# Modulation at one step a half unit beside GLA, one more half unit for the first GLA head, and the DFT table loaded by ScalarE

## The chip, the cores and the metric

The kernel runs on one core of a Trainium2 chip. The metric is the device time of one execution in microseconds (us); smaller is better. TensorE (PE) multiplies, VectorE (DVE) and ScalarE (ACT) work element by element, GpSimd (POOL) and SyncE (SP) here mostly issue DMAs. All engines run at the same time, each through its own list of instructions in order, and wait for each other by semaphores.

## The reference, cut to what matters

One layer of a hybrid diffusion backbone on 384 tokens (128 of context, 256 latent) of width 2048, in float32:

```python
mod = silu(cond) @ w_ada + b_ada          # six maps: shift, scale, gate, twice
h = rmsnorm(x) * (1 + sc1) + sh1
q, k, v, g, lr_f, lr_b, fo = split(h @ w_in)
o = gla(q, k, v, decay(lr_f)) + flip(gla(flip ..., decay(lr_b)))   # 4 heads, 6 chunks of 64
o = rmsnorm(o) * norm * silu(g)
f = real(fft2(fo))                         # over positions and 256 channels, 4 groups
g_a, g_b = split(sigmoid(h @ w_gate + b_gate))
m = (g_a * (o @ w_br_gla) + g_b * (f @ w_br_four)) @ w_out
x = x + ga1 * rmsnorm(m)
h = rmsnorm(x) * (1 + sc2) + sh2
x = x + ga2 * rmsnorm((silu(h @ w_ffn_gate) * (h @ w_ffn_up)) @ w_ffn_down)
```

Two of the six modulation maps are made at the start; the other four (adaLN, `w_ada`) are made beside the matrix products.

## The kernel before

Activations lie transposed, 16 blocks of 128 features by 384 tokens. To keep float32 accuracy, every weight tile (`raw`, 128x1024) is split in two: ScalarE casts it to `whi` (L301; L292 and L295 for special tiles), and VectorE subtracts to get `wlo` (L288, with the shared `TENSOR_TENSOR` operation). A product is then three matmuls (L327: hi by hi, hi by lo, lo by hi). A **half unit** is one weight tile's worth of them: 24 matmuls. A projection of 128 output columns is two half units (`proj`). `grab()` takes the next split pair and, by `push()`, starts the loads and the split of a later one, so that the split runs some half units ahead; `depth[0]` says how many loads lie ahead.

The order on PE, ACT, DVE and POOL is the order in which the code is written; SP is not in that schedule, and its loads are issued as soon as a buffer is free. Work beside the products is written as generators, advanced by `step(side)` once a half unit:

- `gla()`: the scan of each of 4 heads, cut in some 14 steps: `kr`/`krs`, `z` and the log-decay `la` split into `lah`, `lal` (L379/L380), `bT` (L835) and its exponentials, `ki` (L852), the scores `at` (L875), the states `dl`, the outputs `po` (L789), with per-head sums of squares. After the last head, `rs` is taken (L941, L942) and the output is scaled (L946, twelve small operations in three steps).
- `ada_rest()`: the modulation maps in 6 parts. Each part takes 16 weight steps: POOL loads `adaw` (512 KB, 2 buffers), and DVE adds it into `adacc` with two operations (L708; L706 for the first). Then one empty step and one in which PE sums over partitions (`pr`, L719, 8 matmuls). While `on_pe[0]` is set, a weight step is instead four matmuls on PE (L698).
- `run_after()`: 14 turns beside the last seven gate projections (i = 25 to 31), the **folding stage**: sums and differences of token columns for the Fourier branch (`t` L727, `r` L732/L733, ACT copy L728, `hF` L739/L741), and weights of the Fourier columns, folded in place by DVE (L257, L258), with 16 matmuls a tile from the fourth turn on (`pfo`, L1040/L1041).
- in the following stage the output-gate columns ("o"), the DFT and the Fourier branch's projection (`four`, `pf` L1240/L1241) alternate; then come the merge ("a" and "b" tiles), `w_out`, norms and the feed-forward network.

`paced(gen, rate)` advances the modulation `rate[0]` steps a call; in the stage with q, k and 25 gate projections the rate is 1.07. `low_later` delays the `wlo` of a plain weight tile until the next split: DVE then does the folding work first. `cd` is the table of cosines and sines for the DFT (128x1934, 967 KB, L1063), first read by the `pp` matmuls (L1130) in the stage after. In the stage "o" a step of modulation is taken in turns 0 to 5 and then every second turn, on PE from turn 6; in the merge, `TAIL` names the "a" tiles with a step (True: on PE).

Of the kernel before, what the change touches and what calls it, by code (L numbers as in the profile page):

```python
# [37 lines left out]
XU = 2  # L38
GF = 25
GD = 256  # L40
TAIL = {1: True, 4: False, 5: True, 8: True, 10: False, 11: True, 14: False}
RATE = 1.07


C_TRI = 0
# [7 lines left out]
C_CE = C_SEL3 + 96  # L53
# [3 lines left out]
NC = C_CT + 2 * (HT + HL)  # L57
# [51 lines left out]
def tile_step(ctx: ExitStack, tc: tile.TileContext, a, o):  # L109
    nc = tc.nc  # L110
    PE, ACT, DVE, POOL, SP = nc.tensor, nc.scalar, nc.vector, nc.gpsimd, nc.sync
# [137 lines left out]
    low_later = [False]  # L249
# [61 lines left out]
    def take():  # L311
        return ready.pop(0)
# [371 lines left out]
    on_pe = [False]  # L684
# [50 lines left out]
    def over_parts(k, r, low):  # L735

        hi, lo = (hF[k // 4][:, k % 4 : k % 4 + 2, n, :] for n in range(2))
        if low:
            DVE.tensor_sub(lo, r, hi.bitcast(F32))  # L739
        else:  # L740
            ACT.copy(hi, r)  # L741
# [9 lines left out]
    rate = [1.0]  # L751
    ada_gen = ada_rest([(m, half) for m in (2, 3, 4) for half in range(2)])
    ada = paced(ada_gen, rate)
    with ExitStack() as s:
# [22 lines left out]
        def chunks(x):  # L777
            return x.rearrange("p (t c i) -> p t c i", t=3, c=2)

        def gla():  # L780
# [10 lines left out]
            for h in range(NH):  # L791
# [34 lines left out]
                yield  # L826
                if h == 0:
                    yield
                for d in range(2):


                    bT = pss.tile([P, T], F32, tag="side", name="bT")
                    for t in range(3):
                        for j, l in enumerate((lah, lal)):
                            PE.matmul(  # L835
                                bT[:, t * P : (t + 1) * P], l[:, t, d], tri[:, d * P : (d + 1) * P],
                                start=j == 0, stop=j == 1,
                            )
                    sx = pss.tile([P, 2, P], F32, tag="side", name="sx")
                    for j, l in enumerate((lah, lal)):  # L840
                        PE.matmul(
                            sx, tri[:, (2 + d) * P : (3 + d) * P], l[:, 0 : 2 + d : 1 + d, d], start=j == 0, stop=j == 1,
                        )
                    eb = pg.tile([P, T], F32, tag=f"eb{d}", name="eb")
                    ACT.activation(eb, bT, AF.Exp)
                    ki = pg.tile([P, T], F32, tag=f"ki{d}", name="ki")
                    ACT.activation(ki, bT, AF.Exp, scale=-1.0)
                    ko = pg.tile([P, 2, P], F32, tag=f"ko{d}", name="ko")
                    ACT.activation(ko, sx, AF.Exp)
                    qi = pg.tile([P, T], F32, tag=f"qi{d}", name="qi")  # L850
                    DVE.scalar_tensor_tensor(qi, eb, DK**-0.5, qT[:, h, :], op0=ALU.mult, op1=ALU.mult)
                    DVE.tensor_mul(ki, ki, kT[:, h, :])  # L852
                    DVE.tensor_mul(ko, ko, krs[:, 0 : 2 + d : 1 + d, :])

                    last = 0 if d else CH - 1
                    tot = chunks(eb)[:, :, d, last : last + 1]
                    kc = pg.tile([P, 3, CH], F32, tag=f"kc{d}", name="kc")
                    DVE.tensor_mul(kc, chunks(ki)[:, :, d, :], tot.to_broadcast([P, 3, CH]))
                    dc = pg.tile([P, 1], F32, tag=f"dc{d}", name="dc")
                    c = 5 if d else 2  # L860
                    e0, e1 = c * CH + last, (c + 1 - 2 * d) * CH + last
                    DVE.tensor_mul(dc, eb[:, e0 : e0 + 1], eb[:, e1 : e1 + 1])
                    qin.append(qi)
                    kin.append(ki)
                    kcr.append(kc)
                    kout.append(ko)
                    dec.append((tot, dc))
                    yield
# [100 lines left out]
        def side():  # L969
            while True:  # L970
                next(gl, None)
                next(ada, None)
                yield

        sd = side()
        rate[0] = RATE
        for i in qk_order[1:]:
            proj(psm, hT, keep(qk, i), sd)

# [35 lines left out]
    cd = px.tile([P, 2 * G], F32, tag="cd", name="cd")[:, 0 : NC - C_CE]  # L1015
    with ExitStack() as s:
        more = s.enter_context(tc.tile_pool(name="more", bufs=1))
        hF = [actp.tile([P, 4, 2, T], F32R, tag=t, name="hF") for t in ("C_lo", "B_hi", "B_lo")]
        hF.append(more.tile([P, 4, 2, T], F32R, tag="hF", name="hF"))
        sums, folds = [], {}  # L1020

        def ends(n):
            t, r = (more.tile([P, 2, T], F32, tag=z, name=z) for z in ("t", "r"))
            over_ends(2 * n, t, r)
            over_parts(2 * n, r, False)
            folds[n] = r

        def across_n(h, n):
            if n == 0:
                sums[:] = [pss.tile([P, 2, hi - lo], F32, tag="side", name="pfo") for _ in range(2) for lo, hi, _ in parts]  # L1030
            w = take()
            push()
            w_of = [x.rearrange("p (g i k c) -> p i k g c", g=2, i=2, k=2) for x in w]
            for k in range(2):
                kt = 2 * n + k
                x = hF[kt // 4][:, kt % 4]
                for g in range(2):
                    for i, (lo, hi, _) in enumerate(parts):
                        p = sums[2 * g + i]
                        PE.matmul(p, w_of[0][:, i, k, g, :], x[:, :, lo:hi], start=kt == 0, stop=False)  # L1040
                        PE.matmul(p[:, 0], w_of[1][:, i, k, g, :], x[:, 0, lo:hi], start=False, stop=kt == KT - 1)  # L1041
            if n == 7:
                for g in range(2):
                    X.append(px.tile([P, T], F32, tag="yb", name="X", bufs=4))
                    for i, (lo, hi, _) in enumerate(parts):
                        p = sums[2 * g + i]
                        ACT.copy(X[-1][:, lo:hi], p[:, 1])
                        DVE.tensor_add(X[-1][:, lo:hi], X[-1][:, lo:hi], p[:, 0])

        def run_after():  # L1050
            for at, todo in enumerate(after):
                for what, *n in todo:
                    if what == "ends":
                        ends(*n)
                    elif what == "parts":
                        over_parts(2 * n[0], folds.pop(n[0]), True)
                    else:
                        if n == [1, 5]:
                            depth[0] = 2
                            spare_raws.clear()  # L1060
                        across_n(*n)
                if at == turns // 2:
                    SP.dma_start(cd, a["consts"][:, C_CE:NC])  # L1063
                if at in (turns - 4, turns - 3, turns - 1):
                    next(ada_gen, None)
                yield

        ra = run_after()
        low_later[0] = True
        for i in range(GF, 32):  # L1070
            proj(psm, hT, gate(more, i), ra)
            if i == GF:
                depth[0] = 4
                spare_raws.extend([lambda: more.tile([P, G], F32, tag="raw3", name="raw3", bufs=2)] * 2)
        catch_up()
        low_later[0] = False
        depth[0] = 0
        xq = px.tile([P, HT], F32, name="xq")
        POOL.memset(xq, 0.0)
        qb = pss.tile([P, HT], F32, tag="side", name="pfq")  # L1080
        for kb in range(0, KT, 4):
            for x_ in range(2):
                for k in range(kb, kb + 4):
                    q = 32 * (k % 4)
                    PE.matmul(
                        qb[q : q + 4, :], wq[:, k, :], hF[k // 4][:, k % 4, x_, 0:HT].bitcast(F32),
                        start=kb == 0 and x_ == 0, stop=kb == KT - 4 and x_ == 1,
                    )
        for q in range(0, P, 32):
            ACT.copy(xq[q : q + 4, :], qb[q : q + 4, :])  # L1090
# [3 lines left out]
    with ExitStack() as s:  # L1094
# [83 lines left out]
        turn = [0]  # L1178

        def side():  # L1180
            while True:
                on_pe[0] = turn[0] > 5
                if turn[0] < 6 or turn[0] % 2:
                    next(ada_gen, None)
                on_pe[0] = False
                turn[0] += 1
                next(df, None)
                next(nw, None)
                yield
# [71 lines left out]
        for b, i in mix_order:  # L1261
# [18 lines left out]
            else:  # L1280
# [3 lines left out]
                if i == KT - 3:  # L1284
                    depth[0] = 2
                    spare_raws.clear()
                if i in TAIL:
                    on_pe[0] = TAIL[i]
                    next(ada_gen, None)
# [810 lines left out]
```

## Time and profile before

| | us |
|---|---|
| median of 3 runs (lowest, highest) | 1955.28 (1954.93, 1955.28) |
| the profiled execution's own time | 1954.75 |
| its span in the trace | 1953.0 |
| PE busy in the span | 1923.8 (99%) |
| DVE busy | 1650.9 (85%) |
| ACT busy | 915.7 (47%) |
| POOL busy | 85.8 (4%) |

By stages (PE busy of the stretch): start to 142 us: 133.7 of 135; q, k and 25 gate projections with GLA, 142 to 443: 296.8 of 301; folding stage, 443 to 548: 100.8 of 105 (DVE 91.7); stage "o", 548 to 670: 121.3 of 122; merge and `w_out`, 670 to 880: all of 210; the rest, 880 to 1953: 1058.5 of 1073.

A row of the timeline has the start and duration in us, engine, line, operation, output <- input, shapes and count; in brackets stands how long the engine was idle before it and what ended that. The chain of waits has start, duration, and what. In a table of windows, the column after the engines' busy times is the granted clock of TensorE (PEclk, 1 is full), then the DMA engines' share and their rate.

### The profile page before, as it was taken

Reading aid. Unit: us, or ns where it says so; the run is one execution under the profiler, and the core shown is the slowest. Engines: PE = TensorE matmul, PEld = TensorE weight load, DVE = VectorE, ACT = ScalarE, POOL = GpSimd, SP = SyncE. Lnnn points to the kernel's source line nnn. Section 1 sums busy time; section 2 is a strip of 40 time slices with the busy share of each in tenths; the row PEclk is TensorE's granted clock in tenths of the full one; section 3 lists DMA queues with packets and bytes.
Section 4 is the critical chain, followed back from the end, with each engine's and each line's share of the span. In section 5 each row is a group of like instructions: output and inputs, shape, how many; then the busy total and the mean of one; then the engine's idle time right before and its main releaser. Section 6 shows DMA issues by size and latency. Waiting matters only on the chain.

```text
span 1953.0 us, 27535 instructions
## 1 busy us (share of the span) xinstructions
PE 1923.8 (99%) x10526; PEld 1692.8 (87%) x10526; DVE 1650.9 (85%) x2174; ACT 915.7 (47%) x1298; POOL 85.8 (4%) x154
## 2 busy tenths in 40 slices
PE   8999999999999999999999999999999999999997
PEld 5779999999999999999988888888888888888876
DVE  5668898989868897987789898999998999888885
ACT  4235445544455644456454444444444444444444
POOL 0001111110000000004000000000000000000001
PEclk9999999999999999999999999999999999999999
DMA  9977766766556895656254635363636263625243
GB/s 390 387 257 240 252 223 230 261 233 219 181 161 227 297 310 190 222 195 220 81 176 148 189 109 190 126 207 110 205 109 215 93 221 92 200 76 183 86 168 112
DMA packets 200615, 380.52 MB, mean 195 GB/s; under 512 B 14196, under 2 KB 126932, under 8 KB 196132
## 3 DMA queue, kind: packets, MB, share of 16 engines
q1 hardware_dynamic: 181396, 321.83, 48.7%
q0 software_dynamic: 13952, 50.39, 8.5%
q10 hardware_dynamic: 5136, 6.56, 0.9%
q8 instruction: 82, 1.34, 0.3%
q14 instruction: 49, 0.40, 0.1%
HBM read 361.94 MB, written 16.78 MB: 194 GB/s over the span
## 4 chain that ended last, share of the span: by engine, by line
PE 71%; DVE 3%; DMA 1%; ACT 1%; issue 0%; ACTq 0%; DVEq 0%; SPq 0%
PE pgu L339 30%; PE pdn L339 18%; PE pmm L327 17%; PE pf L1240 1%; PE pmm L1517 1%; PE pfo L1040 1%; PE ptr L1809 1%; PE pf L1241 1%; DMA raw<-in_w_d 0%; DMA raw<-in_w_gate 0%; PE pfo L1041 0%; DVE adacc L708 0%; DVE x1b L1961 0%; DMA raw<-in_w_in 0%; PE pr L698 0%
## 5 line engine op out<-in xcount | busy, mean ns | idle before, releaser
L327 PE MATMUL pmm<-A_hi,wlo 128*128 128x384 f32 x1072 | 360.0, 336 | 4.2 <-DVE wlo L288 4.2
L327 PE MATMUL pmm<-A_hi,whi 128*128 128x384 f32 x1072 | 362.8, 338 | 0.0
L327 PE MATMUL pmm<-A_lo,whi 128*128 128x384 f32 x1072 | 359.6, 335 | 0.0
L1664 ACT CAST whi<-u 128x1024 fp32r<-128x1024 f32 x200 | 210.6, 1053 | 281.6 <-DVE u L1648 86.2
L1664 ACT CAST whi<-raw 128x1024 fp32r<-128x1024 f32 x175 | 184.2, 1052 | 202.0 <-PE pgu L339 59.4
L1675 DVE TENSOR_TENSOR wlo<-u,whi 128x1024 fp32r<-128x1024 f32 x200 | 244.3, 1222 | 31.5 <-ACT whi L1664 17.9
L339 PE MATMUL pgu<-whi,A_hi 128*128 128x512 f32 x640 | 250.0, 391 | 0.0
L339 PE MATMUL pgu<-whi,A_lo 128*128 128x512 f32 x640 | 249.3, 389 | 0.0
L1675 DVE TENSOR_TENSOR wlo<-raw,whi 128x1024 fp32r<-128x1024 f32 x175 | 213.7, 1221 | 38.5 <-ACT whi L1664 30.8
L288 DVE TENSOR_TENSOR wlo<-raw,whi 128x1024 fp32r<-128x1024 f32 x163 | 198.3, 1220 | 25.8 <-ACT whi L301 24.4
L301 ACT CAST whi<-raw 128x1024 fp32r<-128x1024 f32 x149 | 155.9, 1050 | 120.8 <-PE pmm L327 57.2
L327 PEld LDWEIGHTS pmm<-A_hi,wlo 128*128 128x128 f32 x1072 | 202.1, 188 | 4.9 <-DVE wlo L288 4.9
L327 PEld LDWEIGHTS pmm<-A_hi,whi 128*128 128x128 f32 x1072 | 202.1, 188 | 3.4 <-issue 2.5
L708 DVE SCALAR_TENSOR_TENSOR adacc<-adaw,spad,adacc 128x1024 f32<-128x1024 f32 x162 | 200.6, 1280 | 2.4 <-DMA adaw<-in_w_ada 1.9
L327 PEld LDWEIGHTS pmm<-A_lo,whi 128*128 128x128 f32 x1072 | 202.2, 189 | 0.2
L339 PE MATMUL pdn<-whi,hid_hi 128*128 128x512 f32 x480 | 186.9, 389 | 0.0
L339 PE MATMUL pdn<-whi,hid_lo 128*128 128x512 f32 x480 | 186.8, 389 | 0.0
L339 PE MATMUL pgu<-wlo,A_hi 128*128 128x512 f32 x640 | 184.2, 389 | 0.0
L339 PEld LDWEIGHTS pgu<-whi,A_hi 128*128 128x128 f32 x640 | 120.2, 188 | 26.1 <-issue 0.8
L339 PEld LDWEIGHTS pgu<-wlo,A_hi 128*128 128x128 f32 x640 | 120.1, 188 | 25.4
L339 PEld LDWEIGHTS pgu<-whi,A_lo 128*128 128x128 f32 x640 | 120.1, 188 | 25.0
L339 PE MATMUL pgu<-whi,S 128*128 128x512 f32 x480 | 131.1, 395 | 0.0
(405 smaller groups left out, 3042.7 us busy)
## 6 DMA issues: line engine op xcount, KB each, us to landing
adaw<-in_w_ada POOLq DMA_DIRECT2D x96, 512.0 KB, 3.9
raw<-in_w_d SPq DMA_DIRECT2D x88, 512.0 KB, 3.7
slab<-in_w_ada SPq DMA_DIRECT2D x32, 1024.0 KB, 10.0
raw<-in_w_gate SPq DMA_DIRECT2D x64, 512.0 KB, 4.6
raw<-in_w_g SPq DMA_DIRECT2D x48, 512.0 KB, 3.5
raw<-in_w_u SPq DMA_DIRECT2D x48, 512.0 KB, 3.6
raw<-in_w_in SPq DMA_DIRECT2D x44, 512.0 KB, 4.2
u<-in_w_u SPq DMA_DIRECT2D x40, 512.0 KB, 4.7
```

The costliest lines, as they stand in the source:

```text
L288: eng.tensor_sub(lo, raw, hi.bitcast(F32))
L301: ACT.copy(hi, raw)
L327: PE.matmul(dst, w[wi][:, k * n + n0 : k * n + n0 + P], x[xi][:, k0 + k, :], start=first and k == 0 and j == 0, stop=last and k == kts - 1 ...
L339: PE.matmul(dst, stat[x_][m], mov(w[w_], m), start=first and w_ == m == x_ == 0, stop=last and w_ == m == 1,)
L708: DVE.scalar_tensor_tensor(acc[:, c, :], w, spad[:, k, c : c + 1], acc[:, c, :], op0=ALU.mult, op1=ALU.add,)
L1040: PE.matmul(p, w_of[0][:, i, k, g, :], x[:, :, lo:hi], start=kt == 0, stop=False)
L1240: PE.matmul(pf[:, 0 : 2 * HT], w[0][:, c], x[k], start=k == 0, stop=False)
L1241: PE.matmul(pf[:, 0:HT], w[1][:, c], x[k][:, 0:HT], start=False, stop=m == 1 and k == 3)
L1517: PE.matmul(hp[u], hw[u][j][:, ((k - 1) % 8) * P : ((k - 1) % 8 + 1) * P], h2[m][:, k - 1, :], start=k == 1 and j == m == 0, stop=k == KT ...
L1664: ACT.copy(hi, src)
L1675: DVE.tensor_sub(lo, src, hi.bitcast(F32))
L1809: PE.transpose(pt[:, j, :], src[:, j * P : (j + 1) * P], ident)
```

## The change

- `RATE` goes: beside GLA the modulation takes one step a half unit.
- For head 0 `gla()` takes one more empty step after the split of the log-decay.
- The load of `cd` in turn 7 of the folding stage is issued by ACT, in its program order, instead of by SP.
- `low_later` is set after the first of the seven gate projections instead of before it.
- In the stage "o" the modulation's steps are taken in turns 0 to 8 and then in odd turns; they run on PE from turn 7 on, without turn 8.
- `TAIL` gets a step at tile 13 (on PE) and one at 15 (on DVE).

Counted over the program, there are 87 calls of the modulation ahead of `w_out` before and after; one of the weight steps more is on PE (10 instead of 9) and one fewer on DVE.

```diff
-TAIL = {1: True, 4: False, 5: True, 8: True, 10: False, 11: True, 14: False}
-RATE = 1.07
+TAIL = {1: True, 4: False, 5: True, 8: True, 10: False, 11: True, 13: True, 14: False, 15: False}
@@ gla()
                 split_act(lah, lal, la)
                 yield
                 if h == 0:
+                    yield
                     yield
@@
         sd = side()
-        rate[0] = RATE
         for i in qk_order[1:]:
             proj(psm, hT, keep(qk, i), sd)
@@ run_after()
                 if at == turns // 2:
-                    SP.dma_start(cd, a["consts"][:, C_CE:NC])
+                    ACT.dma_start(cd, a["consts"][:, C_CE:NC])
@@
         ra = run_after()
-        low_later[0] = True
         for i in range(GF, 32):
             proj(psm, hT, gate(more, i), ra)
             if i == GF:
                 depth[0] = 4
+                low_later[0] = True
                 spare_raws.extend([lambda: more.tile([P, G], F32, tag="raw3", name="raw3", bufs=2)] * 2)
@@ side() of the stage "o"
-                on_pe[0] = turn[0] > 5
-                if turn[0] < 6 or turn[0] % 2:
+                on_pe[0] = turn[0] > 6 and turn[0] != 8
+                if turn[0] < 9 or turn[0] % 2:
                     next(ada_gen, None)
```

Three places show how this moves instructions. First DVE, where the stage with GLA ends and the folding stage begins (L946 scales the GLA output; `raw` under L257 and L258 is the first Fourier weight). Before:

```order
L946 TENSOR_SCALAR qk<-qk,rs 128x2x128 x4
L708 SCALAR_TENSOR_TENSOR adacc<-adaw,spad,adacc 128x1024 x2
L946 TENSOR_SCALAR qk<-qk,rs 128x2x128 x4
L727 TENSOR_TENSOR t<-A_hi,A_lo 128x768
L732 TENSOR_TENSOR r<-t 128x2x64
L733 TENSOR_TENSOR r<-t 128x2x63
L732 TENSOR_TENSOR r<-t 128x2x128
L733 TENSOR_TENSOR r<-t 128x2x127
L257 TENSOR_TENSOR raw<-raw 128x2x256
L258 SCALAR_TENSOR_TENSOR raw<-raw 128x2x256
L288 TENSOR_TENSOR wlo<-raw,whi 128x1024
L739 TENSOR_TENSOR hF<-r,hF 128x2x384
```

After (line numbers in this part of the program are one smaller, except in `gla`):

```order
L707 SCALAR_TENSOR_TENSOR adacc<-adaw,spad,adacc 128x1024 x2
L946 TENSOR_SCALAR qk<-qk,rs 128x2x128 x8
L287 TENSOR_TENSOR wlo<-raw,whi 128x1024
L726 TENSOR_TENSOR t<-A_hi,A_lo 128x768
L731 TENSOR_TENSOR r<-t 128x2x64
L732 TENSOR_TENSOR r<-t 128x2x63
L731 TENSOR_TENSOR r<-t 128x2x128
L732 TENSOR_TENSOR r<-t 128x2x127
L256 TENSOR_TENSOR raw<-raw 128x2x256
L257 SCALAR_TENSOR_TENSOR raw<-raw 128x2x256
L738 TENSOR_TENSOR hF<-r,hF 128x2x384
```

The GLA output is finished one half unit later, and the `wlo` that stood behind the first turn's sums and the first fold now stands ahead of the first `t`.

Second, the load of `cd`. On SP before, at the start of the folding stage, ahead of a gate's weights:

```order
L235 DMA raw_4617<-in_w_in 128x4x256
L235 DMA raw_4619<-in_w_gate 128x1024
L1063 DMA cd<-in_consts 128x1934
L235 DMA raw<-in_w_gate 128x1024
L235 DMA raw<-in_w_in 128x4x256
```

On ACT after, in turn 7, some 40 us later in the program:

```order
L300 CAST whi<-raw_4810 128x1024
L727 COPY r<-t 128x2x2
L740 CAST hF<-r 128x2x384
L1062 DMA cd<-in_consts 128x1934
L259 COPY wq<-raw_4842 128x2x2
L291 CAST whi<-raw_4842 128x1024
L982 ACTIVATE gz<-pmm,bgate 128x384
```

SP's row is gone, and behind ACT's row stand the casts of a Fourier weight and of the next gate.

Third, ACT in the stage with GLA, at the log-decay of head 2 (`la`; `gz` is a finished gate tile, stored by the DMA behind it). Before:

```order
L301 CAST whi<-raw 128x1024
L983 ACTIVATE gz<-pmm,bgate 128x384
L984 DMA gates_d<-gz 128x384
L819 ACTIVATE la<-z 128x512
L819 ACTIVATE la<-z 128x256
L820 ACTIVATE la<-la 128x768
```

After:

```order
L300 CAST whi<-raw 128x1024
L982 ACTIVATE gz<-pmm,bgate 128x384
L983 DMA gates_d<-gz 128x384
L300 CAST whi<-raw 128x1024
L818 ACTIVATE la<-z 128x512
L818 ACTIVATE la<-z 128x256
```

Since every later GLA step of heads 0 to 3 falls one half unit later, the gate's `gz` and its DMA now stand one cast ahead of `la` instead of right ahead of it.

## Prediction

> **What bounds the kernel.** I read the page's engine shares first, then TensorE's waits, then the timeline at each long one, and for the longest the chain of waits and the granted clock.
>
> ```profile
> PE 1923.8 (99%) x10526; PEld 1692.8 (87%) x10526; DVE 1650.9 (85%) x2174; ACT 915.7 (47%) x1298; POOL 85.8 (4%) x154
> ...
> PE pmm L327 <- DVE wlo L288: 4.2, 2, 3.7
> ```
>
> PE is busy for 1923.8 of 1953.0 us. The change leaves the matmuls nearly as they are, so it can gain only from PE's waiting (29 us in all) and from time in which PE's clock is low. PE's longest wait in the stages that change is the 3.7 us for a `wlo`. These are the others there:
>
> ```profile
> 189.72 0.57 PE L875 MATMUL at<-qi,ki 128*64 128x64 f32 x12 [1.76 <-DVE ki L852]
> ...
> 223.98 0.64 PE L719 MATMUL pr<-adacc,selr 128*32 128x256 f32 x8 [0.91 <-DVE adacc L708]
> 225.18 0.64 PE L719 MATMUL pr<-adacc,selr 128*32 128x256 f32 x8 [0.56 <-DVE adacc L708]
> ...
> 317.15 0.33 PE L835 MATMUL bT<-cg,lal 128*128 128x128 f32 x1 [0.37 <-DVE lal L380]
> 384.16 0.33 PE L835 MATMUL bT<-cg,lal 128*128 128x128 f32 x1 [0.56 <-DVE lal L380]
> ...
> 532.34 0.44 PE L327 MATMUL pmm<-A_hi,wlo 128*128 128x384 f32 x1 [0.53 <-DVE wlo L288]
> 595.90 0.36 PE L1241 MATMUL pf<-edT,wlo 128*128 128x194 f32 x1 [0.66 <-DVE wlo L288]
> ```
>
> The long one lies at the start of the folding stage. Here are rows of the chain of waits, in order of time, and then three windows:
>
> ```profile
> 447.17 1.05 DVE qk L946 x4
> ...
> 451.71 1.23 DVE wlo L288
> ...
> 453.00 7.61 DMA raw<-in_w_gate
> ...
> 464.84 1.23 DVE wlo L288
> ...
> 466.12 6.67 PE pmm L327 x22
> ```
>
> ```profile
> 462.40:464.94 2.54, 0.00 (x1) 0.00 (x0) 2.07 (x5) 1.13 (x3) 0.00 (x0) 1.00 0.21 77
> 464.94:471.76 6.82, 5.64 (x18) 5.64 (x19) 6.75 (x11) 3.35 (x6) 0.00 (x0) 0.50 0.50 154
> ...
> 189.72:196.00 6.28, 6.28 (x54) 6.21 (x55) 6.23 (x10) 0.99 (x2) 0.53 (x1) 1.00 0.66 236
> ```
>
> A gate's weights are issued at 453.00, when the delayed `wlo` of 451.71 has freed their buffer, and land 7.61 us later; their own `wlo` is ready at 466.07. PE stands still from 462.40 to 466.12. After 2.54 us of that its granted clock falls to 0.50 and stays there for 6.82 us. At full clock the matmuls of a half unit follow each other by (602.24 - 601.72) / 3 = 0.173 us, so 24 of them take 4.16:
>
> ```profile
> 601.72 0.33 PE L327 MATMUL pmm<-A_hi,wlo 128*128 128x384 f32 x1
> ...
> 602.24 0.34 PE L327 MATMUL pmm<-A_hi,wlo 128*128 128x384 f32 x1
> 602.51 0.64 PE L698 MATMUL pr<-adaw,spad 128*32 128x256 f32 x8
> 603.08 0.55 PE L1197 MATMUL pt<-ident,qk 128*128 128x128 f32 x3
> ```
>
> The 22 matmuls of the chain's last row took 6.67 us instead of 22 x 0.173 and 0.2 for the last one's end, 4.0: the low clock cost some 2.65. The `at` wait of 1.76 had no such sequel; the window behind it has full clock. So the stop cost 3.7 + 2.65 = 6.4 us.
>
> [...]
>
> **The change, part by part.**
>
> *Rate 1.0, and head 0's empty step.* At 1.07 every fifteenth half unit takes two modulation steps. One step is two DVE operations:
>
> ```profile
> 222.64 2.48 DVE L708 SCALAR_TENSOR_TENSOR adacc<-adaw,spad,adacc 128x1024 f32<-128x1024 f32 x2
> 225.03 1.22 DVE L288 TENSOR_TENSOR wlo<-raw,whi 128x1024 fp32r<-128x1024 f32 x1
> ```
>
> Operations overlap by 0.09, so the pair takes 2.39 and with `wlo` a half unit asks DVE for 2.39 + 1.13 = 3.52 us, where PE takes 4.16. GLA's own operations come on top. The `at` wait is DVE running late in head 0, and one more half unit ahead of it lets DVE catch up 4.16 - 3.52 = 0.64. I take -0.65; the ends are 0 and -1.76. The two `pr` waits come when the last L708 pairs of a part are late; without a double step ahead of them they come one half unit earlier against PE: -1.47, or 0 if DVE is late for another reason. The `bT` waits follow the log-decay on ACT:
>
> ```profile
> 376.24 0.57 ACT L983 ACTIVATE gz<-pmm,bgate 128x384 f32<-128x384 f32 x1
> ...
> 377.22 0.87 ACT L819 ACTIVATE la<-z 128x512 f32<-128x512 f32 x2 [0.40 <-ACT gz L983]
> ```
>
> ```profile
> 381.16 1.02 DVE L823 SCALAR_TENSOR_TENSOR la<-z,la 128x512 f32<-128x512 f32 x2 [0.42 <-ACT la L821]
> ```
>
> `gz` and its DMA move one cast ahead, so `la` can start 377.22 - 376.24 = 0.98 sooner. DVE waited only 0.42 at L823, so the 0.56 falls by 0.42, and the 0.37 goes: -0.8. The two instructions now stand ahead of other GLA steps on ACT. I price that at 0, since DVE has four pairs of 2.39 fewer in this stage; the other end is +1.5, 0.98 at one head and half of it at another. The stage: -2.9.
>
> *Folding stage.* GLA ends a half unit later, and all behind it on DVE. On ACT the end of GLA was:
>
> ```profile
> 434.61 0.37 ACT L936 COPY qk<-po 128x256 f32<-128x256 f32 x1 [3.56 <-PE po L789]
> ...
> 435.24 1.05 ACT L301 CAST whi<-raw 128x1024 fp32r<-128x1024 f32 x1
> ...
> 437.17 1.28 ACT L941 ACT_TABLE_LOAD   x1 [0.39 <-ACT gz L983]
> ```
>
> The copy of the last `po` moves by 4.16 to 438.77. Behind it come 0.63 until the cast, 1.05, 1.28 and 0.3 for `rs`, which is ready at 442.0. Then on DVE: L942 0.25, L946 four times 1.05, the pair 2.39, L946 eight times 2.1, and the `wlo` that is no longer delayed, 1.23. So the first `t` starts at 449.1 or 449.2, against 448.31 before. That `wlo` frees the buffer: the gate's load goes out near 449.2 instead of 453.00. The chain on from the first `t`:
>
> ```profile
> 448.31 0.96 DVE L727 TENSOR_TENSOR t<-A_hi,A_lo 128x768 f32<-128x768 f32 x1
> ...
> 453.72 0.95 DVE L727 TENSOR_TENSOR t<-A_hi,A_lo 128x768 f32<-128x768 f32 x1
> ...
> 457.79 0.95 DVE L727 TENSOR_TENSOR t<-A_hi,A_lo 128x768 f32<-128x768 f32 x1
> ```
>
> The first turn took 5.41 and takes 4.27 without its `wlo` (1.14 with the overlap), the second 4.07. From the third `t` to the end of the critical `wlo` it is as from the first `t` to the `wlo` of 451.71: 3.40, and 1.23. The end is 449.2 + 4.27 + 4.07 + 4.63 = 462.2, and PE needs it at 462.4: the wait goes, with 0.2 us to spare. The cast is early enough if the weights land by 456.5, 7.3 us after their issue; before they took 7.61, but with the 967 KB of `cd` right ahead of them. A sum of a dozen rounded rows can be off by more than 0.2, so I leave 0.5 us of wait, between 0 and 1.0. A wait of 1.0 is below the 1.76 that left the clock alone. Term: -6.4 + 0.5 = -5.9.
>
> *`cd` on ACT.*
>
> ```profile
> 449.32 1.57 SPq L1063 DMA_DIRECT2D cd<-in_consts  x1
> ...
> 494.91 1.22 DVE L288 TENSOR_TENSOR wlo<-raw,whi 128x1024 fp32r<-128x1024 f32 x1
> ...
> 502.88 0.25 PE L1041 MATMUL pfo<-hF,wlo 128*128 128x194 f32 x1
> ...
> 453.00:461.00 8.00, 8.00 (x49) 8.00 (x48) 6.20 (x11) 1.36 (x3) 0.31 (x1) 1.00 1.01 357
> 485.00:500.00 15.00, 15.00 (x94) 15.00 (x93) 14.83 (x26) 8.07 (x14) 0.00 (x0) 1.00 0.53 169
> ```
>
> The issue kept SP for 1.57 us and will keep ACT as long, at about 492 us, ahead of a Fourier weight's cast and the next gate's. That Fourier weight's `wlo` was ready at 496.13, 6.7 us before PE's first use at 502.88: hidden, and +1.6 if this cover were gone. The bytes move from a stretch where the DMA engines are full (1.01) to one where they are half empty (0.53): at the 357 - 169 = 188 GB/s to spare 967 KB take 5.1 us, while up to four loads lie ahead and the table is first read in the next stage. Price 0.
>
> [...]
>
> *Stage "o" and the merge.* The pair of turn 5 goes:
>
> ```profile
> 590.08 2.48 DVE L708 SCALAR_TENSOR_TENSOR adacc<-adaw,spad,adacc 128x1024 f32<-128x1024 f32 x2
> ...
> 594.62 1.23 DVE L288 TENSOR_TENSOR wlo<-ws,whi 128x1024 fp32r<-128x1024 f32 x1 [0.40 <-ACT whi L295]
> ```
>
> It lies right ahead of the `wlo` for which PE waited 0.66 at 595.90: -0.66. Turns 7 and 8 get 0.3 and 1.4 us of DVE work, less than the 2.39 that leaves; +0.6 if that isn't covered. The step that moves to PE costs 603.08 - 602.51 = +0.57. In the merge PE does not wait, so tiles 13 and 15 are 0. The wait at 532 stays.
>
> **Sum.** -2.9 - 5.9 - 0.66 + 0.57 = -8.9. The profiled execution took 1954.75 (its span and 1.75 us around it), 0.5 below the median of the runs. From it the sum gives 1945.9, from the median 1955.28 - 8.9 = 1946.4, which I forecast. All ends taken together make it 1944.8 to 1952.7.
>
> **The rivals.**
> 1. *The stop moves but stays* (0.17). If the chain or the weights come 2.4 us later than summed, PE waits 2.5 us and more, and the clock halves as before. Then -5.9 becomes 0 to -1.2, and the time 1951.1 to 1952.3. For it: DVE has no gap in this chain. Against: the landing has time in hand.
> 2. *Slower: DVE stays behind in the folding stage* (0.11). It is busy for 91.7 of 105 us there, and the stop had given it 6.4. It decides from a lateness of 2.5 us at tile after tile: each is then a stop with a halved clock, 6.4 us. Two of them less the 9.4 gained elsewhere and at the old stop make 1958.7, three 1965. Against: behind the stop DVE came 6.7 us ahead of PE again (the rows at `cd`), and loses 6.4 - (466.07 - 462.2) = 2.5 of that.
> 3. *GLA turns tight* (0.11): ACT's new order brings a wait of 1 to 3 us at a head: 1947.4 to 1949.4.
> 4. *The low clock isn't the stop's doing* and stays (0.04): 1949.1.
> 5. Something that these rows don't show, at a loss (0.05). The forecast itself has 0.52.
>
> **Numbers.** 0.2% (3.9 us) is about what a measurement of this kernel can tell from no change. Faster than 1951.4 are the forecast, the third, the fourth and a third of the first: 0.73. Within 0.2% lie the rest of the first and half of the second: 0.16. Slower: the other half and the fifth, 0.11. The range, 1943.5 to 1953, holds all but the second and the fifth.
>
> **What would show it.** In the changed profile: no PE wait over 2 us and full clock from 455 to 480; the gate's load issued some 4 us sooner; the `at` wait near 1.1, none for `pr` near 225, `bT` waits of 0.2 at most; 1.57 us of ACT for `cd` and no PE wait behind it; no `pf` wait near 590; ten steps at L698. The forecast is wrong if PE still waits over 2.5 us where folding begins, or anew at the states or scores of heads 1 to 3.

## The result and the profile after

The changed kernel takes 1942.42 us (median of 4 runs, 1941.85 to 1943.09), the kernel before 1955.11 (1954.72 to 1955.28): a ratio of 0.9937, 95% interval 0.9921 to 0.9953, 12.7 us less. Forecast were 8.9 us less and a range that ended at 1943.5. The direction was right, the size too small, and the time lies 1.1 us below the range.

The page of the changed kernel, and its list of TensorE's waits (total, times, longest):

```profile
PE 1920.4 (99%) x10534; PEld 1690.8 (87%) x10534; DVE 1647.8 (85%) x2172; ACT 916.3 (47%) x1298; POOL 85.8 (4%) x154
```

```profile
PE px L394 <- ACT spad L522: 4.1, 1, 4.1
PE py L1949 <- DVE ep L2007: 1.8, 1, 1.8
PE at L875 <- DVE ki L852: 1.5, 1, 1.5
PE pmm L1516 <- ACT A_hi L1478: 0.5, 1, 0.5
```

Of the waits in the changed stages only `at` is left: no `pmm`, `pr`, `bT` or `pf` wait over 0.15 us. Windows around the old stop (clock at 1.00 throughout), then SP, DVE and PE there:

```profile
455.00:458.40 3.40, 3.40 (x25) 3.23 (x23) 3.37 (x8) 2.04 (x4) 0.00 (x0) 1.00 0.48 169
458.40:465.00 6.60, 6.60 (x42) 6.48 (x41) 6.53 (x11) 3.20 (x6) 0.00 (x0) 1.00 0.54 159
```

```profile
445.51 0.81 SPq L234 DMA_DIRECT2D raw<-in_w_gate  x2
...
457.12 1.22 DVE L287 TENSOR_TENSOR wlo<-raw,whi 128x1024 fp32r<-128x1024 f32 x1
...
458.21 0.33 PE L326 MATMUL pmm<-A_lo,whi 128*128 128x384 f32 x1
458.40 0.44 PE L326 MATMUL pmm<-A_hi,wlo 128*128 128x384 f32 x1
```

The row of SP holds two loads; the second is the critical one, and it goes out at 445.90 instead of 453.00. Its `wlo` ends at 458.34, and PE reads it at 458.40, 0.19 us behind the matmul ahead of it, against 0.17 in a run without a wait: just in time.

Where the time went, by the start of the same PE matmul in both traces (us; the profiled spans are 1953.0 and 1940.4):

| place | before | after | difference | this stretch |
|---|---|---|---|---|
| first stage | 37.84 | 37.67 | -0.17 | -0.2 |
| end of GLA | 438.60 | 434.92 | -3.68 | -3.5 |
| at the old stop | 462.06 | 458.21 | -3.86 | -0.2 |
| end of the low clock | 471.72 | 461.45 | -10.27 | -6.4 |
| behind the wait at 532 | 532.62 | 521.57 | -11.05 | -0.8 |
| behind the wait at 596 | 596.09 | 583.94 | -12.15 | -1.1 (0.25 of it only moved) |
| merge, the added PE step behind it | 732.11 | 720.83 | -11.28 | +0.9 (with the 0.25) |
| near the end of the feed-forward network | 1894.86 | 1883.29 | -11.57 | -0.3 |
| behind a wait at 1896 | 1902.32 | 1889.76 | -12.55 | -1.0 |

### The profile page after: what moved, and what is told of

It reads as the page before. It is cut to its first block, busy times and chain, and to the rows that moved or that the text cites. A ratio compares the mean times of both kernels' runs of the same rounds, so it can differ in the third digit from the quotient of the medians.

```text
span 1940.4 us, 27538 instructions
## 1 busy us (share of the span) xinstructions
PE 1920.4 (99%) x10534; PEld 1690.8 (87%) x10534; DVE 1647.8 (85%) x2172; ACT 916.3 (47%) x1298; POOL 85.8 (4%) x154
## 4 chain that ended last, share of the span: by engine, by line
PE 93%; DVE 3%; DMA 2%; issue 1%; ACT 1%; SPq 0%; DVEq 0%; ACTq 0%
PE pgu L338 30%; PE pmm L326 30%; PE pdn L338 18%; PE pv L491 3%; PE pgm L474 1%; PE pf L1239 1%; PE pfo L1039 1%; DVE adacc L707 1%; PE pmm L1516 1%; PE ptr L1808 1%; PE pf L1240 1%; PE pfo L1040 1%; DMA xraw<-in_w_x 1%; PE po L788 1%; PE px L509 0%
```

## The experiments

The theory: the stop at the start of folding is a buffer that the delayed `wlo` holds; the halves of the change add up. Rivals: `cd`'s bytes make the stop; or it goes only together with the lighter DVE.

**The two halves.** The folding half is the kernel before with these edits:

```diff
-                    SP.dma_start(cd, a["consts"][:, C_CE:NC])
+                    ACT.dma_start(cd, a["consts"][:, C_CE:NC])
-        low_later[0] = True            # ahead of the seven gates
+                low_later[0] = True    # behind the first of them
```

> The kernel before with two parts of the change alone: the later low_later and cd on ACT; GLA, stage o and merge as before. Theory A (the stop at the start of folding is the gate's weights that come late, by the buffer that the delayed wlo holds and by cd's bytes; the parts add up): the stop of 3.7 us and the low clock go, also the wait of 0.5 near 532, the waits beside GLA stay: 1955.1 - 6.9 = 1948.2, within 1947.5 to 1949.5. Theory B (the stop goes only together with GLA's later end and the lighter DVE): a stop of over 2.5 us with low clock stays, 1954 to 1955.

Measured: 1948.24 (1945.95 to 1949.85) against 1954.15 (1952.25 to 1957.44) on that chip; ratio 0.9964 (0.995 to 0.9979), -5.9, one us less than I had expected. The wait near 532, which I had expected to go too, was 1.36 in this trace. The other half is all other lines of the diff (rate, `yield`, turns of stage "o", `TAIL`):

> The other half: rate 1.0, head 0's empty step, stage o and merge as changed; low_later and cd as before. Theory A: the waits beside GLA go (-3.5 by the two traces), the wait of 0.66 near 596 goes, one step more on PE (+0.57), the stop of 3.7 and the low clock stay: 1951.5, within 1950.5 to 1952.5. Theory B: the stop goes here, since DVE is lighter ahead of it: about 1945.

Measured: 1949.1 (1948.3 to 1950.02), ratio 0.9972 (0.9961 to 0.9983), -5.0. PE's wait at the stop, first in the folding half, then in the other:

```profile
462.52 0.44 PE L327 MATMUL pmm<-A_hi,wlo 128*128 128x384 f32 x1 [0.68 <-DVE wlo L288]
```

```profile
462.15 0.69 PE L327 MATMUL pmm<-A_hi,wlo 128*128 128x384 f32 x1 [3.71 <-DVE wlo L288]
```

The folding half alone removes the stop and the low clock, the other leaves both as they were: the 22 matmuls from that one on took 4.11 us in the first and 6.36 in the other, against 6.67 in the kernel before. The second half gave more than the 3.6 that I had expected. The whole change was measured twice more:

> The whole change again, beside its parts on one chip. Theory A (the parts add): what the folding half alone gained (1948.24 against 1954.15, -5.9) and what the GLA half alone gained (-5.0) together, -10.9 against before, within -10 to -13. Theory B (they overlap or hinder each other): clearly less than the sum, -8.

> The whole change once more, as the yardstick of the two kernels beside it: -10.6 to -12.7 against before, as in its two measurements so far.

Measured: 1943.37 against 1953.97 (ratio 0.9945, 0.9929 to 0.9962), and 1942.52 against 1954.94 (0.9937, 0.9922 to 0.9952): -10.6 and -12.4. The halves' sum is -10.9: they add, within a spread of 2 us between chips.

**Buffer or bytes.** Each edit of the folding half alone, on the kernel before, and each undone alone, on the changed kernel.

> The kernel before with the later low_later alone. Theory A1 (the held buffer is the cause): the gate's load goes out near 449, ahead of cd, and lands by 455: no stop, 1948.2 to 1949.5. Theory A2 (cd's bytes and SP's 1.57 us are the cause): cd still shares the engines with it, a stop of 2.6 us or more stays, with the low clock: 1952 to 1955.

> The kernel before with cd on ACT in turn 7 alone. Theory A1 (the held buffer): the load still goes out at 453.0; with fewer bytes beside it, it may land up to 2.6 us sooner (967 KB at 370 GB/s), so the stop is 1.1 us or more; at 1.1 with full clock 1949.8, at 3.7 unchanged 1955. Theory A2 (cd): the load lands in its usual 4.2 to 4.6 us, at 457.5, no stop: 1948.2 to 1949.

> The changed kernel with low_later set before the first folding gate again; the rest as changed. Theory A1 (the buffer held by the delayed wlo makes the stop): the gate's load goes out some 3.4 us later again, PE stops for 2 to 3.7 us and the clock halves for one or two periods of 3.4 us: 3.5 to 6.4 us slower than the changed kernel. Theory A2 (with cd away and a lighter DVE the delay is harmless): within 1 us of the changed kernel.

> The changed kernel with cd loaded by SP again; it then stands two loads behind the critical gate's weights. Theory A1 (the held buffer): same as the changed kernel, within 1 us; PE's wait for the critical wlo under 1 us. Theory A2 (cd's bytes beside the gate's load count): the load lands 1 to 2.6 us later, PE waits as long and the clock may halve: 1 to 5 us slower than the changed kernel.

| kernel | median (runs) | before there | ratio (interval) | PE's wait at the critical `wlo` |
|---|---|---|---|---|
| before with the later `low_later` | 1948.91 (1946.69 to 1950.39) | 1954.15 | 0.9971 (0.996 to 0.9983) | 0.23 |
| before with `cd` on ACT | 1952.55 (1949.54 to 1954.18) | 1954.15 | 0.999 (0.9981 to 1.0) | 2.94 |
| changed, `low_later` back | 1945.8 (1944.97 to 1946.74) | 1953.97 | 0.9957 (0.9942 to 0.9972) | 2.28 |
| changed, `cd` on SP | 1943.06 (1942.42 to 1944.58) | 1953.97 | 0.9944 (0.9929 to 0.9959) | none |

In the last two the yardstick is the changed kernel's 1943.37 on the same chip: +2.4 and -0.3. So the buffer was the cause, and where `cd` is loaded makes no difference that can be measured once `low_later` is right. SP's loads say why; before with the later `low_later`, then with `cd` moved:

```profile
448.14 0.81 SPq L235 DMA_DIRECT2D raw<-in_w_gate  x2
449.01 0.42 SPq L1063 DMA_DIRECT2D cd<-in_consts  x1
```

```profile
449.73 4.56 SPq L235 DMA_DIRECT2D raw<-in_w_gate  x2
```

```profile
453.95 6.21 DMA raw<-in_w_gate
```

In the first, the critical load (the second of the two) stands ahead of `cd` and leaves at 448.53. In the second its issue still waits for the buffer until 453.95, and with `cd` out of its way it takes 6.21 us, which the chain of waits shows, instead of 7.61. In the other half alone, with `cd` ahead of it as before, it took 7.95. So by two traces of each kind `cd`'s bytes were worth 1.4 to 1.8 us of landing, not the 2.6 that I had put in that expectation, and the 1.6 us that moving `cd` alone gave have an interval that reaches no change. With `low_later` back in the changed kernel the stop was 2.28 and the loss 2.4, less than the 3.5 to 6.4 expected, since the load again took 6.18 and the clock was low for a shorter time (0.50 from 460.17 to 463.59; the 22 matmuls behind the wait took 5.50 instead of 6.67).

**Head 0's step.**

```diff
                 if h == 0:
-                    yield
                     yield
```

> The changed kernel without head 0's added empty step: GLA's steps stand at the half units where they stood before, at rate 1.0. Theory A (the lighter rate does most): the at wait of head 0 grows by up to 0.7, the bT waits may come back (0.4 and 0.6), pr's stay away: 0.5 to 1.7 us slower than the changed kernel. Rival (the step costs as much as it saves): same within 0.5, since GLA then ends a half unit earlier and the first t of the folding stage comes 0.9 us sooner.

Measured: 1944.64 (1943.75 to 1946.45), +1.3 on the changed kernel beside it. The trace of it has this, and no other wait in the stage:

```profile
190.05 0.57 PE L874 MATMUL at<-qi,ki 128*64 128x64 f32 x12 [2.32 <-DVE ki L851]
```

The `at` wait is longer here than in the seven traces of kernels that have both the step and the rate of 1.0 (0.84 to 1.61; 1.03, 1.44 and 1.55 in the three of the changed kernel). That fits a gain of about 1 us from the step, but it is one trace, and the runs overlap with those of the changed kernel beside it (1942.01 to 1945.28). `bT` has no wait here although `gz` and its DMA stand right ahead of `la` as before. So in this trace the rate of 1.0 is enough, and my reason for the end of those waits, the order on ACT, is not needed.

**How tight the chain is.** The critical `wlo` is computed three times over:

```diff
             def low():
-                eng.tensor_sub(lo, raw, hi.bitcast(F32))
+                lows[0] += 1
+                for _ in range(3 if lows[0] == 68 else 1):
+                    eng.tensor_sub(lo, raw, hi.bitcast(F32))
```

> The changed kernel with the critical wlo of the folding stage computed three times over, 2 x 1.13 = 2.26 us more DVE work at that place and nothing else. Theory A (that wlo is just in time, with 0.2 us or less to spare): PE waits 2.1 to 2.3 us for it; 2.1 to 2.3 slower than the changed kernel at full clock, up to 3.9 to 5.6 if the clock halves for one or two periods of 3.4 us. Rival (there is slack, or the next stretch gives it back): under 1 us slower. On the clock: theory F (it halves by the share of a free running window of 3.41 us in which PE stood still, half or more) has it halve in some executions and not in others; theory L (a fixed length of stop, below 2.3 us) has it halve always.

Measured: 1946.15 (1944.65 to 1946.87) against the changed kernel's 1942.52: +3.6. PE waits for the whole addition of 2.26 and a little more, and the clock is at 0.50 for 3.42 us:

```profile
460.80 0.69 PE L329 MATMUL pmm<-A_hi,wlo 128*128 128x384 f32 x1 [2.37 <-DVE wlo L290]
```

```profile
457.29:460.70 3.41, 1.14 (x8) 0.83 (x6) 3.34 (x4) 1.88 (x2) 0.00 (x0) 1.00 0.00 0
460.70:464.12 3.42, 3.32 (x10) 3.32 (x11) 3.38 (x7) 0.20 (x1) 0.00 (x0) 0.50 0.54 161
```

There is no slack in the chain: the forecast's 0.2 to spare was right to within that. Of the two theories on the clock, the fixed length does not hold: the stop of 2.32 without head 0's step left the clock at 1.00, and one of 1.75 was followed by 0.50 (last section). These four runs alone, 2.1 to 4.4 above the changed kernel, don't show in which of them it fell.

**Taking away the last wait.** Two versions leave out the modulation step right ahead of head 0's second `ki`; one gives it back in the merge, the other beside head 1's last products.

```diff
                 next(gl, None)
-                next(ada, None)
+                if sdn[0] != 6:                               # first version; TAIL gets 12: False
+                    next(ada, None)
+                for _ in range({6: 0, 29: 2}.get(sdn[0], 1)): # second version, TAIL as changed
+                    next(ada, None)
+                sdn[0] += 1
```

> The changed kernel without the modulation step right ahead of head 0's second ki (2.39 us of DVE), and one step more at tile 12 of the merge, on DVE. Theory A (DVE's lateness in head 0 makes the at wait of 1.0 to 1.5): the wait goes and nothing takes its place: 1.0 to 1.5 us faster than the changed kernel. Rival (the modulation's later phase brings waits elsewhere, at pr or in stage o): same or slower.

> The changed kernel without the modulation step right ahead of head 0's second ki, and with two steps instead of one beside the last products of head 1, where DVE waits for a load; from there on the modulation stands at the half units of the changed kernel, so stage o and the merge are untouched. Theory A: the at wait of 1.0 to 1.5 us goes as in the kernel with the step moved to the merge, and the pf wait of 0.6 near 582 that came there does not come: 1.5 to 2 us faster than the changed kernel, -12 to -14.5 against before. Rival (the double step makes DVE late for head 2's log-decay): a bT wait of 0.4 to 1 us near 318, no better than with the step in the merge.

Measured: the first 1940.98 (1940.56 to 1942.32), ratio 0.993 (0.9916 to 0.9945), beside the changed kernel's 1942.52 (1941.98 to 1942.82); the second 1941.48 (1940.78 to 1942.45), ratio 0.9927 (0.9903 to 0.9952). In both the `at` wait is gone. In their place stand, first version and second:

```profile
581.73 0.36 PE L1243 MATMUL pf<-edT,wlo 128*128 128x194 f32 x1 [0.63 <-DVE wlo L287]
```

```profile
521.67 0.44 PE L326 MATMUL pmm<-A_hi,wlo 128*128 128x384 f32 x1 [1.53 <-DVE wlo L287]
```

The `pf` wait came with the modulation's later phase, as the rival had it, and is absent in the second version, which puts the step back early; it costs less than what was gained. The first version is 1.5 us below the changed kernel beside it. The second ran on another chip, without the changed kernel beside it: it is 13.1 below the kernel before there, where the changed kernel was 12.4 below on its chip. Both differences are at the edge of what these runs tell apart, and the second's is less than the 1.5 to 2 us that I had expected: in its trace the wait of 1.53 takes back what `at` gave.

## Why the prediction fell short

*What held.* The stop was late weights behind a held buffer, its removal brought the full clock back (1.00 from 455 to 480), and with 6.4 us this was half of the gain. The chain from the last `po` to the critical `wlo` came out as summed. The `pr`, `bT` and `pf` waits went, `cd` on ACT cost nothing, the step more on PE cost its 0.6, tiles 13 and 15 nothing. No rival came true: neither a new stop, nor a DVE that stays behind, nor a new wait at a head.

*What failed.* The step that failed is the sum, which is 3.7 us short of the 12.6 in the two traces. Of these, 2.3 came from places that it put at nothing: 1.3 behind `w_out`, 0.8 in the stretch of the wait at 532, 0.2 in the first stage, which the change doesn't touch. The other 1.4 are terms taken too small: 0.7 at the old stop, 0.6 beside GLA, 0.1 in the stage "o" and the merge. Term by term:
- "I leave 0.5 us of wait": there was none. The term of -5.9 measured -6.6 with the 0.2 ahead of it.
- "The wait at 532 stays": it went, -0.5, and that was luck as far as the traces show. I had taken a wait for a load as a constant of the kernel. In the chain of waits of the kernel before, and of the second version above:

```profile
523.75 5.95 DMA raw<-in_w_in
```

```profile
512.08 6.95 DMA raw<-in_w_in
```

  In every trace with a wait of over 0.1 there, PE was ready for this load's `wlo` 8.06 us after the load's issue, so the wait is what the landing takes beyond some 5.4 us. The landing took 5.0, 5.7 and 4.8 us in the three traces of the changed kernel (waits of 0, 0.24 and 0). With waits of 1.36 in the folding half alone, 1.26 in the other half and 1.53 in this version, nothing shows that the change removed it.
- GLA, -2.9: it measured -3.5. `at` fell by 0.2 instead of 0.65; it lies between 0.7 and 1.8 in the four traces with the old GLA part. `pr` and `bT` went, 1.5 and 0.9 by the idle times in brackets. By the starts of the matmuls they had held PE up longer, some 1.75 and 1.25: the `bT` of 317.15 started 0.59 behind the matmul ahead of it, where the changed kernel has 0.06, and the bracket says 0.37, since it counts from that matmul's modelled end. The remaining 0.3 is not attributed. The `pr` waits are also absent in one trace with the old GLA part (`cd` moved alone), so not all of this need be the change's doing. The `bT` term was too small, and its reason, the order on ACT, not needed.
- Stage "o", -0.66: right. But 1.3 us came behind `w_out`, which the sum doesn't have. Most of it is a wait of 0.67 at 1896, which stands in the traces of before and of the three kernels that have its modulation, and in none of the ten others:

```profile
1896.18 0.66 PE L1809 MATMUL ptr<-ident,ep 128*128 128x128 f32 x4 [0.67 <-DVE ep L1802]
```

  SP's order at the end of `w_out` differs in the same way (a load of `w_g` ahead of a last one of `w_out`, or behind it). In all fourteen traces the two go together, but that this is the cause wasn't tried and stays open.
- The price of 1.57 us for issuing `cd` was not the issue's: SP took 0.42 for it in the trace above and ACT 0.37 in the changed kernel. What held SP in the trace of before stays open; nothing hung on it.

The range was too narrow below because its ends came only from the terms that I had listed: all their good ends together made 1944.8, and the 1.3 us that I allowed beyond that had no source. All but `at` came out near their good end or better, and two waits that I had called fixed or had not listed went as well. In one of the two repeats the gain was 10.6 instead of 12.7, so some of the miss is also spread between measurements.

## What to carry to other kernels

A subtraction that is put off by one step also puts off the release of its input buffer, and so the load that waits for the buffer: here it left at 453.00 instead of 448.53, and the cost showed two half units later as a late load, on another engine. The landing of one load differed by 0.9 us between three executions of one kernel, and the wait for it by up to 1.5 us between kernels that are alike there, so read such a wait from several traces before it is called a constant. When several short waits lie in the stages that a change touches, let the range's good end take them all.

## What the runs showed of the hardware

In these runs the halving of TensorE's clock did not go by the length of a stop. In the trace of before it is at 0.50 from 464.94 to 471.76 and from 1946.32 on, behind the last matmul, and at 1.00 between; (471.76 - 464.94) / 2 is 3.41 and (1946.32 - 471.76) / 432 is 3.413. In the changed kernel's it falls once, at 1934.31, behind the last matmul. These windows are cut at multiples of the same 3.41 us from the first full clock of each trace; in order, `at` waiting 1.76 (before), 2.32 (no second step for head 0) and 1.75 (`cd` moved alone):

```profile
188.46:191.87 3.41, 2.15 (x31) 2.12 (x31) 3.41 (x8) 0.69 (x2) 0.13 (x1) 1.00 0.77 264
191.87:195.28 3.41, 3.41 (x21) 3.41 (x21) 3.36 (x5) 0.27 (x1) 0.53 (x1) 1.00 0.39 113
```

```profile
185.30:188.71 3.41, 2.42 (x24) 2.04 (x22) 3.41 (x5) 0.97 (x2) 0.59 (x2) 1.00 0.61 241
188.71:192.13 3.42, 2.08 (x30) 2.05 (x31) 3.42 (x8) 0.85 (x2) 0.21 (x1) 1.00 0.77 256
192.13:195.54 3.41, 3.41 (x22) 3.41 (x21) 3.36 (x5) 0.19 (x1) 0.53 (x1) 1.00 0.41 115
```

```profile
186.90:190.31 3.41, 1.66 (x37) 1.30 (x37) 3.41 (x8) 1.42 (x2) 0.80 (x2) 1.00 0.44 118
190.31:193.72 3.41, 3.41 (x18) 3.29 (x13) 3.41 (x4) 0.00 (x0) 0.53 (x1) 0.50 0.52 209
```

The stop of 2.32 was cut in two by a window's end (2.42 and 2.08 us busy), and the clock stayed at 1.00; the one of 1.75 fell into one window (1.66 busy), and the next was at 0.50. Here are these and some other windows cut in this way, each at a clock of 1.00 itself, by PE's idle share; the traces of before and of the changed kernel have no others of 40% or more ahead of the last matmul:

| trace | window | PE busy of 3.41 us | idle | clock of the next |
|---|---|---|---|---|
| before | 188.46 | 2.15 | 37% | 1.00 |
| no second step for head 0 | 188.71 | 2.08 | 39% | 1.00 |
| before | 222.59 | 1.94 | 43% | 1.00 |
| changed | 190.10 | 1.86 | 45% | 1.00 |
| before | 1936.08 | 1.84 | 46% | 1.00 |
| `cd` moved alone | 186.90 | 1.66 | 51% | 0.50 |
| changed | 1924.07 | 1.59 | 53% | 1.00 |
| step moved to the merge | 1922.90 | 1.55 | 55% | 0.50 |
| changed, `low_later` back | 456.76 | 1.43 | 58% | 0.50 |
| critical `wlo` three times | 457.29 | 1.14 | 67% | 0.50 |
| before | 461.52 | 0.88 | 74% | 0.50 |

In these eleven the clock stayed at 1.00 up to 46% and was at 0.50 from 55% on; between them the window of 51% was followed by 0.50 and the one of 53% by 1.00. At 0.50, the window of 464.94 in the trace of before was idle for 35%, and the next was at 0.50 too; behind the next, busy throughout (468.35), the clock was back at 1.00, as it was behind such a window with `cd` moved alone (190.31, busy throughout) and behind one with the critical `wlo` three times (460.70, 3.32 busy). So stops of 1.75, 2.28, 2.37 and 3.7 us were followed by a halved clock, and stops of 1.76 and 2.32 were not: what differs between 1.75 and 1.76 is how the windows cut them. My own reading, that a wait of 1.76 leaves the clock alone, held for the one wait it was taken from.

In five measurements the median of the kernel before lies between 1953.97 and 1955.11, and its single runs between 1952.25 and 1957.44, with one at 1962.03. The mean granted clock was 0.994 in that one and 0.996 or 0.997 in the six runs beside it; whether stops and their phase make this spread was not shown, since there is no trace of those runs.
